# Storing one expert's result in sixteen row blocks instead of three, in a one-core mixture-of-experts kernel on Trainium2

## The chip, the cores and the metric

The kernel runs on one core of one Trainium2 chip. Its time is that of one execution on the device, in microseconds. Before the change two timed runs took 182.07 and 181.54 us, with a median of 181.81. The core has five engines with instruction streams of their own: TensorE (PE, whose weight loads are shown as PEld), VectorE (DVE), ScalarE (ACT), GpSimd (POOL) and SyncE (SP). Transfers run on 16 DMA engines that the core's queues share; SyncE, ScalarE and GpSimd issue them.

## The reference

Eight experts, each a two-layer network on its own 256 tokens, all in float32:

```python
n_experts, capacity, hidden, expert_hidden = 8, 256, 512, 2048
h = np.matmul(x, w1) + b1[:, np.newaxis, :]
h = np.maximum(h, 0)
return (np.matmul(h, w2) + b2[:, np.newaxis, :]).astype(np.float32)
```

The output is 8 x 256 x 512 floats, 512 KB for each expert.

## The kernel before

The work goes expert by expert. `first_product` (line 114) computes the hidden layer of an expert in 16 blocks of 128 units, four matmuls each (line 121), and ScalarE applies bias and ReLU on the way out of PSUM (line 128). `second_product` (line 166) runs three experts later (`LAG = 3`): for each of the two token blocks a bias matmul with a row of ones (line 171) and 16 matmuls (line 178). Experts 6 and 7 (`HALVED`) take their second weights in two halves of 1 MB, so that the products of the first half can start before the second has landed.

The weights are loaded as float16 by GpSimd's queue, which casts on the way (lines 84 and 93). The order of GpSimd's issues is written out by hand in a list, `ring` (lines 215 to 225), and is the order in which its queue moves data: activations, first weights, second weights, and at the end, behind the last weights, the grouped stores (`flush`, line 138).

`store` (line 142) copies an expert's two PSUM blocks to SBUF, one by VectorE (line 156), one by ScalarE (line 157). Each of the 128 rows of the tile is 4 KB, contiguous in the output. Where the result goes from there depends on the expert:

- Experts 0 to 3 and experts 4 and 5 are gathered in two tiles, which GpSimd's queue stores at the end in one transfer of 2 MB and one of 1 MB (line 140).
- Expert 6 is stored at once, in the row ranges that the table `PARTS` (line 40) gives: rows 0 to 25 by SyncE, 25 to 121 by ScalarE, 121 to 128 by SyncE (line 164).
- Expert 7, which is not in the table, is stored by SyncE in one transfer of 128 rows (line 164).

Instructions of one engine run in the order of the program. On ScalarE the copy of expert 7 (line 157) stands behind the issues for expert 6 (line 164); on SyncE the store of expert 7 stands behind those of expert 6. The two loads of the first two experts' activations (line 190) are SyncE's as well. The framework that builds the kernel gives the transfers of SyncE and ScalarE eight semaphores in turn; when one comes round again, the issue waits for the transfer that had it before.

Of the kernel before, what the change touches and what calls it, by code (L numbers as in the profile page):

```python
# [10 lines left out]
def kernel(  # L11
# [12 lines left out]
    E, T, H = x.shape  # L24
    M = w1.shape[2]
    P = 128
# [10 lines left out]
    HALVED = (E - 2, E - 1)  # L37


    PARTS = {E - 2: ((0, 25, False), (25, 121, True), (121, 128, False))}  # L40
    nXF32 = 2
    X_LOADS = {2: 2, 4: 4}

# [98 lines left out]
    def store(e, po):  # L142
# [16 lines left out]
        if e in group_of:  # L159
            if e == first + n - 1:  # L160
                pending[first] = (dst, out_sb)
            return
        for p0, p1, scalar in PARTS.get(e, ((0, P, False),)):
            (nc.scalar if scalar else nc.sync).dma_start(out=dst[p0:p1], in_=out_sb[p0:p1])
# [101 lines left out]
```

## Time and profile before

| | |
|---|---|
| time, median of two runs | 181.81 us (181.54 to 182.07) |
| span of the profiled execution, first to last instruction | 179.8 us (no other time is recorded for it) |
| mean granted TensorE clock | 0.932 |
| HBM read and written | 71.39 MB and 4.19 MB, 420 GB/s over the span |
| DMA packets | 3828, of them 460 under 512 B |
| costliest group: first product, line 121 | 512 matmuls, 64.9 us busy |
| second product, line 178 | 256 matmuls, 60.0 us busy |
| copies of results, lines 156 and 157 | 22 each, 15.1 and 12.7 us busy |

How to read the views that follow: the page lists busy time by engine and cuts the span into 40 slices, each digit a busy share in tenths. The queue rows give packets, megabytes and the time that the packets took as a share of 16 engines' span; q0 is GpSimd's queue, q1 SyncE's and q10 ScalarE's. The chain of waits gives start, duration and what ran or was waited for, in order of time. The DMA view lists issues with size and the time from issue to landing; it can be cut to a stretch of time, and its shares are then shares of that stretch. The windows give busy time of each engine, the granted clock, the DMA share and GB/s for chosen stretches. Times in the views count from the span's start.

### The profile page before, as it was taken

What the parts mean: (1) busy time and instruction counts of PE and PEld (TensorE: products, weight loads), DVE (VectorE), ACT (ScalarE), POOL (GpSimd) and SP (SyncE); (2) the same over time, 40 slices, a digit from 0 to 9 for tenths busy, and PEclk for the clock granted to TensorE, in tenths of its full rate; (3) what the DMA queues carried; (4) which work ended last, traced back from release to release, by engine and by line L of the source; (5) the groups of instructions that cost most, each with busy time, mean ns of one, the idle gap of its engine ahead of it and who ended that gap; (6) DMA issues with size and microseconds to landing.
All of it is one profiled execution on the core that took longest, in us unless ns stands there. A gap on an engine that the chain in (4) does not pass through costs nothing.

```text
span 179.8 us, 1957 instructions
## 1 busy us (share of the span) xinstructions
PE 129.0 (72%) x784; PEld 86.2 (48%) x784; DVE 87.8 (49%) x125; ACT 70.2 (39%) x151; POOL 13.4 (7%) x28
## 2 busy tenths in 40 slices
PE   0005199959995930999869597969788887999740
PEld 0004089948993410794369244943387433343310
DVE  1999933985000199999999998000600020301010
ACT  0000569947993050482189005940298020111010
POOL 7000003020201010001000001000100020020000
PEclk9999999987999995599999799996999999999995
DMA  5999999999999999999999999999999999999995
GB/s 215 252 230 195 233 208 201 233 228 200 215 231 193 219 230 222 197 226 230 208 204 230 219 200 226 230 211 200 230 219 201 226 211 208 217 211 221 324 456 215
DMA packets 3828, 40.56 MB, mean 226 GB/s; under 512 B 460, under 2 KB 476, under 8 KB 1132
## 3 DMA queue, kind: packets, MB, share of 16 engines
q0 software_dynamic: 3232, 38.35, 96.5%
q1 hardware_dynamic: 476, 1.70, 2.4%
q10 hardware_dynamic: 112, 0.39, 0.5%
q8 instruction: 6, 0.10, 0.2%
q14 instruction: 2, 0.02, 0.0%
HBM read 71.39 MB, written 4.19 MB: 420 GB/s over the span
## 4 chain that ended last, share of the span: by engine, by line
DMA 55%; PE 32%; ACT 3%; another core or an unknown queue 3%; POOL 2%; issue 1%; POOLq 0%; ACTq 0%
DMA w1sb<-in_w_dram 43%; PE po L178 16%; PE ph L121 15%; DMA w2sb<-in_w_dram 12%; ACT out L157 3%; PE po L171 1%; POOL w1sb L84 1%; ACT hT L128 1%; POOL w2sb L93 0%; POOL x L76 0%; POOL b_sb L192 0%; POOL b_rows L196 0%; POOLq L250 0%; ACTq L128 0%
## 5 line engine op out<-in xcount | busy, mean ns | idle before, releaser
L121 PE MATMUL ph<-xT,w1sb 128*128 128x256 f16 x512 | 64.9, 293 | 34.1 <-DMA w1sb<-in_w_dram 21.5
L121 PEld LDWEIGHTS <-w1sb 128*128 128x128 f16 x512 | 59.8, 147 | 40.1 <-DMA w1sb<-in_w_dram 31.8
L178 PE MATMUL po<-w2sb,hT 128*128 128x512 f16 x256 | 60.0, 394 | 9.8 <-DMA w2sb<-in_w_dram 9.8
L112 DVE STREAM_TRANSPOSE xT<-x 32x256 f16<-32x256 f16 (+1 forms) x64 | 53.0, 888 | 26.0 <-DMA x<-in_x_dram 19.2
L128 ACT ACTIVATE hT<-ph,b1T 128x256 f16<-128x256 f32 x128 | 56.2, 474 | 14.4 <-PE ph L121 14.2
L178 PEld LDWEIGHTS <-hT 128*128 128x128 f16 x256 | 25.5, 101 | 44.1 <-issue 17.8
L156 DVE COPY out<-po 32x512 f32<-32x512 f32 (+2 forms) x22 | 15.1, 688 | 53.7 <-PE po L178 53.5
L157 ACT COPY out<-po 32x512 f32<-32x512 f32 (+2 forms) x22 | 12.7, 579 | 68.8 <-PE po L178 68.6
L109 DVE STREAM_TRANSPOSE xT<-x 32x256 f16<-32x256 f16 x32 | 14.0, 436 | 0.5
L93 POOL DMA_DIRECT2D w2sb<-in_w_dram x10 | 5.3, 534 | 71.6 <-PE po L178 71.6
L84 POOL DMA_DIRECT2D w1sb<-in_w_dram x8 | 4.8, 601 | 64.1 <-PE ph L121 63.3
L128 ACT ACT_TABLE_LOAD x1 | 1.3, 1283 | 20.1 <-DVE b1T L208 20.1
L171 PE MATMUL po<-b_sb,ones 1*128 1x512 f16 x16 | 4.8, 379 | 0.0
L208 DVE STREAM_TRANSPOSE b1T<-b_rows 32x512 f32<-32x512 f32 x4 | 4.1, 1031 | 0.1
L201 DVE CAST x<-x 128x1024 f16<-128x1024 f32 x2 | 1.4, 694 | 3.1 <-DMA x<-in_x_dram 3.1
L171 PEld LDWEIGHTS <-ones 1*128 1x128 f16 x16 | 0.9, 92 | 2.1 <-issue 2.1
L140 POOL DMA_DIRECT2D out_dram<-out x2 | 1.1, 538 | 9.8 <-ACT out L157 9.8
L76 POOL DMA_DIRECT2D x<-in_x_dram x2 | 1.1, 552 | 0.0
L197 DVE MEMSET ones<- 1x128 f16 x1 | 0.2, 165 | 0.8 <-PEq L250 0.8
L196 POOL DMA_DIRECT2D b_rows<-in_b_dram x1 | 0.5, 515 | 0.0
L192 POOL DMA_DIRECT2D b_sb<-in_b_dram x1 | 0.5, 513 | 0.0
L250 POOL MEMSET const-float32-0.0<- 128x1 f32 x1 | 0.1, 99 | 0.2 <-issue 0.2
(3 smaller groups left out, 0.3 us busy)
## 6 DMA issues: line engine op xcount, KB each, us to landing
w1sb<-in_w_dram POOLq DMA_DIRECT2D x8, 2048.0 KB, 34.8
w2sb<-in_w_dram POOLq DMA_DIRECT2D x6, 2048.0 KB, 47.2
w2sb<-in_w_dram POOLq DMA_DIRECT2D x4, 1024.0 KB, 23.2
out_dram<-out POOLq DMA_DIRECT2D x1, 2048.0 KB, 19.0
x<-in_x_dram SPq DMA_DIRECT2D x2, 512.0 KB, 3.7
x<-in_x_dram POOLq DMA_DIRECT2D x1, 1024.0 KB, 31.2
out_dram<-out POOLq DMA_DIRECT2D x1, 1024.0 KB, 14.9
x<-in_x_dram POOLq DMA_DIRECT2D x1, 512.0 KB, 24.0
```

The costliest lines, as they stand in the source:

```text
L84: ordered(nc.gpsimd.dma_start(out=w1_sb[e], in_=w1[e].rearrange("(p kc) m -> p kc m", kc=nKC)))
L93: ordered(nc.gpsimd.dma_start(out=w2_sb[e][:, lo : lo + half], in_=src[:, lo : lo + half]))
L109: nc.vector.transpose(out=out[:, :, g, :, 0, :], in_=block[:, :, :, 0, :])
L112: nc.vector.transpose(out=out[:, tb, g], in_=block[:, tb])
L121: ordered(nc.tensor.matmul(out=ph, lhsT=w1_sb[e][:, kc, :].rearrange("p (q j) -> p q j", j=nJ)[:, :, j], rhs=xT[e][:, kc, :], start=(kc == 0),
L128: nc.scalar.activation(out=hT[e][:, j, :].rearrange("p (tb k i) -> p tb k i", tb=nTB, k=split), in_=ph.rearrange("p (tb i k) -> p tb k i", ...
L156: nc.vector.tensor_copy(out=out_sb[at : at + rows, k * nTB, :], in_=po[0][part])
L157: nc.scalar.copy(out=out_sb[at : at + rows, k * nTB + 1, :], in_=po[1][part])
L171: ordered(nc.tensor.matmul(out=t, lhsT=ones1, rhs=b2_sb[0:1, e * H : (e + 1) * H], start=True, stop=False,))
L178: ordered(nc.tensor.matmul(out=po[tb], lhsT=hT[e][:, j, tb * P : (tb + 1) * P], rhs=w2_sb[e][:, j, :], start=False, stop=(j == nJ - 1),))
L201: nc.vector.tensor_copy(out=t, in_=x32[e])
L208: nc.vector.transpose(out=b1T[b * B : (b + 1) * B, nB - 1 - b : nB - 1 - b + nJ * B], in_=b1_rows.rearrange("r (i j) -> r j i", j=nJ),)
```

## The change

The table entry of expert 6 is replaced. Instead of three transfers of 25, 96 and 7 rows there are sixteen, of 15, 8, 13, 14, 11, 12, 9, 10, 7, 6, 5, 4, 3, 2, 1 and 8 rows, SyncE and ScalarE in turn beginning with SyncE. They cover the same 128 rows in order. In words: the store of expert 6 in sixteen transfers of 1 to 15 rows, so that every DMA engine gets its own count of rows.

```diff
-    PARTS = {E - 2: ((0, 25, False), (25, 121, True), (121, 128, False))}
+    RUNS = ((15, False), (8, True), (13, False), (14, True), (11, False), (12, True), (9, False),
+            (10, True), (7, False), (6, True), (5, False), (4, True), (3, False), (2, True),
+            (1, False), (8, True))
+    PARTS = {E - 2: []}
+    for rows, scalar in RUNS:
+        at = PARTS[E - 2][-1][1] if PARTS[E - 2] else 0
+        PARTS[E - 2].append((at, at + rows, scalar))
+    assert PARTS[E - 2][-1][1] == P
```

Nothing else is edited; lines below the table move down by seven. The built instruction streams of PE, DVE and POOL keep their order. Those of SP and ACT become, from the first store on (rows x elements, and the semaphores of DMA transfers that the issue waits for; semaphores of engines are left out):

```
SP    store 15x1024
SP    store 13x1024
SP    store 11x1024
SP    store  9x1024   waits DMAHW1 (an activation load had it)
SP    store  7x1024   waits DMAHW3 (the 15-row store)
SP    store  5x1024   waits DMAHW5 (the 13-row store)
SP    store  3x1024   waits DMAHW7 (the 11-row store)
SP    store  1x1024   waits DMAHW1 (the 9-row store)
SP    store 128x1024  waits DMAHW2 (the 6-row store), and both copies of expert 7
ACT   store  8x1024
ACT   store 14x1024
ACT   store 12x1024
ACT   store 10x1024
ACT   store  6x1024   waits DMAHW2 (the first 8-row store)
ACT   store  4x1024   waits DMAHW4 (the 14-row store)
ACT   store  2x1024   waits DMAHW6 (the 12-row store)
ACT   store  8x1024   waits DMAHW0 (the 10-row store)
ACT   copy of expert 7's second block, line 157 (before the change it stood behind one store)
```

Which transfer had a semaphore before is read off the order in which the eight are given out. In the kernel before, no issue of a store waited for another transfer.

## Prediction

> **What bounds the kernel now.** I read the page first (busy shares and queues), then the chain of waits for its last steps, then the timeline of the issuing queues, and last the DMA view and the windows over the end.
>
> ```profile
> span 179.8 us, 1957 instructions
> ...
> PE 129.0 (72%) x784; PEld 86.2 (48%) x784; DVE 87.8 (49%) x125; ACT 70.2 (39%) x151; POOL 13.4 (7%) x28
> ...
> DMA  5999999999999999999999999999999999999995
> ...
> q0 software_dynamic: 3232, 38.35, 96.5%
> q1 hardware_dynamic: 476, 1.70, 2.4%
> q10 hardware_dynamic: 112, 0.39, 0.5%
> ...
> DMA 55%; PE 32%; ACT 3%; another core or an unknown queue 3%; POOL 2%; issue 1%; POOLq 0%; ACTq 0%
> ```
>
> The 16 DMA engines are full in every slice but the first and the last; no compute engine is above 72%. GpSimd's queue (q0) fills them with weights, and at the end with two grouped stores. Whatever lengthens the work of the busiest DMA engine, or issues the last transfer later, can move the end.
>
> ```profile
> 147.74 21.57 DMA w2sb<-in_w_dram
> 169.32 0.04 issue
> 169.36 3.63 PE po L178 x16
> 172.99 0.02 issue
> 173.01 0.59 ACT out L157
> ```
>
> The last compute chain: the last weights land at 169.32, 16 matmuls follow, then ScalarE copies the second half of expert 7 from 173.01 to 173.60. SyncE then issues the last store. The DMA view gives the stores and what they took to land, the timeline their issues:
>
> ```profile
> out_dram<-out POOLq DMA_DIRECT2D x1, 2048.0 KB, 19.0
> ...
> out_dram<-out POOLq DMA_DIRECT2D x1, 1024.0 KB, 14.9
> ...
> out_dram<-out SPq DMA_DIRECT2D x1, 512.0 KB, 5.3
> out_dram<-out ACTq DMA_DIRECT2D x1, 384.0 KB, 8.1
> out_dram<-out SPq DMA_DIRECT2D x1, 100.0 KB
> ...
> out_dram<-out SPq DMA_DIRECT2D x1, 28.0 KB
> ```
> ```profile
> L164 SPq DMA_DIRECT2D out_dram<-out x3: 301/358/360, 164.8 to 173.6; - x3
> ...
> L164 ACTq DMA_DIRECT2D out_dram<-out x1: 380/380/380, 164.8 to 164.8; - x1
> ```
>
> Expert 6's three stores are issued from 164.81 on, expert 7's store (512 KB) at 173.60, and it lands 5.3 later, at 178.9. Behind that come 0.9 us of closing steps, so the span ends at 179.8. No separate time of the profiled execution is recorded; the median of the two timed runs, 181.81, is 2.0 us above this span, and I carry that difference over unchanged.
>
> The windows over the end show how level the DMA engines finish (the columns before the last two are empty engines and the clock; the last but one is the DMA share, where a packet counts at its start):
>
> ```profile
> 177.00:178.56 1.56, 0.00 (x0) 0.00 (x0) 0.00 (x0) 0.00 (x0) 0.00 (x0) 0.50 0.57 234
> ```
> ```profile
> 177.20:177.40 0.20, 0.00 (x0) 0.00 (x0) 0.00 (x0) 0.00 (x0) 0.00 (x0) 0.50 0.90 369
> 177.40:177.60 0.20, 0.00 (x0) 0.00 (x0) 0.00 (x0) 0.00 (x0) 0.00 (x0) 0.50 0.65 266
> 177.60:177.80 0.20, 0.00 (x0) 0.00 (x0) 0.00 (x0) 0.00 (x0) 0.00 (x0) 0.50 0.70 287
> 177.80:178.00 0.20, 0.00 (x0) 0.00 (x0) 0.00 (x0) 0.00 (x0) 0.00 (x0) 0.50 0.80 328
> 178.00:178.20 0.20, 0.00 (x0) 0.00 (x0) 0.00 (x0) 0.00 (x0) 0.00 (x0) 0.50 0.27 103
> 178.20:178.40 0.20, 0.00 (x0) 0.00 (x0) 0.00 (x0) 0.00 (x0) 0.00 (x0) 0.50 0.10 41
> 178.40:178.60 0.20, 0.00 (x0) 0.00 (x0) 0.00 (x0) 0.00 (x0) 0.00 (x0) 0.50 0.00 0
> ```
>
> In the last 1.56 us an engine idles 43% of the time: 0.67 us. That is the most that perfect levelling could win. About 11 of 16 engines (0.70) work to 178, five have stopped by 177.6.
>
> **The change, part by part.** It removes three issues (25, 96 and 7 rows) and adds sixteen. Nothing moves on TensorE, VectorE and GpSimd: their built instruction order is the same.
>
> *Rows per engine.* q1's 1.70 MB are 416 rows of 4 KB (256 of the two x loads, 25, 7 and 128); its other 60 packets are small. The three 128-row transfers have 16 small ones each if they behave as q10's 96 rows (112 packets, 16 small); 12 are left, which is 5 + 7: 25 rows went to 5 engines and 7 rows to 7. So a transfer of r rows up to 15 gives one row to each of r engines. If all begin at the same engine, as the change's words have it, the loads were 12 rows on five engines, 7 on two, 6 on nine; they become 16, 15, 14, 13, 12, 11, 10, 9, 7, 6, 5, 4, 3, 2, 1, 0. The Trainium skill ("DMA: Bandwidth & Descriptors", section "Why a DMA increments its semaphore by 16 and not by 1") says that hardware queues take the lowest-numbered engines; no row here names an engine.
>
> *Price of a row.* In the last store's window:
>
> ```profile
> q1 hardware_dynamic: 144, 0.52, 45.8%
> ```
>
> This is 175.80 to 178.60: 45.8% of 16 engines times 2.8 us is 20.5 us, for 128 rows 0.160 us each. The heaviest engine gets 4 rows more, 0.64 us, and 13 more small packets (16 transfers for 3). Their price is not shown; the q10 row below (23.0% of 16 x 4.2 us over 96 rows: 0.161 us) hardly differs, so they lie between 0 and about 0.02 us: 0 to 0.26 in all. Which engines end early decides whether this shows. Starting level, the 11 light engines would end 0.8 to 0.96 us ahead of the five heavy; the windows show 11 late and five early. In the packet records behind these views the early five carry no q1 rows ahead of the last store, so they are light engines, and the heavy five are among the late eleven. These ends lie between about 177.9 and 178.55. The first gets 0.64 to 0.9 more: its new end is 178.55 to 179.45, **0 to +0.9 us**; I take +0.6. The rows taken off the upper engines free partly engines that were early already.
>
> *Issues and their waits.* ScalarE now issues 8 at 0.38 us, SyncE 9 with the last. The built listing says more: four of each go out at once, from 164.81 to 166.3. Each later one waits for the landing of the transfer four places ahead on its own queue (SyncE's 9-row one waits for an x load, long done). Behind ScalarE's last issue stands the copy of 173.01. The last store waits for ScalarE's 6-row transfer. Before, no such wait existed, so I bound it by the rings' pace:
>
> ```profile
> q0 software_dynamic: 107, 0.79, 99.7%
> ```
> ```profile
> q0 software_dynamic: 154, 1.29, 72.3%
> q10 hardware_dynamic: 112, 0.39, 23.0%
> q1 hardware_dynamic: 41, 0.13, 7.7%
> ```
>
> The first is 164.81 to 168.36: for 3.55 us after the issue only q0 moves. The second is 168.30 to 172.50: all 7 packets per engine of q10 pass among q0's. From the landing, (8.1 - 3.55) / 7 = 0.65 us per packet; from the window, 4.1 / 7 = 0.59. I take 0.62. A one-row transfer is two packets, so the n-th of a queue has landed near 168.4 + 1.24 n: 169.6, 170.9, 172.1, 173.4.
> - ScalarE: the 6-row issue goes at 169.6, the last 8-row one at 173.4, done 173.8. The copy starts there and not at 173.01: +0.8, done 174.4.
> - SyncE: its four later issues go at the same marks, the last done by 173.8.
> - The 6-row transfer, issued until 170.0, is fifth on its ring: landing 174.6, or by the issue delay 170.0 + 3.55 + 1.24 = 174.8. So the last store goes at 174.8, **1.2 us late**.
>
> What that costs at the end is bounded by two landings, the loaded 5.3 above and the shortest of the idle x loads:
>
> ```profile
> DMA to landing us min/median/max: 3.3/3.7/4.1
> ```
>
> 174.8 + 3.3 = 178.1 (hidden behind q0's last packets) and 174.8 + 5.3 = 180.1 (+1.2). The cover is q0, which in the old run was still writing the grouped stores when the store was issued:
>
> ```profile
> q0 software_dynamic: 61, 1.00, 105.9%
> ```
>
> That is 173.60 to 175.80, nothing but q0. An issue in 174.8 comes as q0 runs dry, so it is nearer the idle end: I take 4.6, which is 179.4, +0.5.
>
> *A rule against the change.* The Trainium skill ("DMA: Bandwidth & Descriptors", "Anatomy of one DMA" and "Rules for kernel authors") puts a fixed cost near 2.0 us on every DMA and says to merge what is under 64 KB. Fully in series, eight on ScalarE would be 16 us by its figure, and the copy would begin about 181, an estimate that adds some 8 us. The rows say that packets of one ring follow at 0.6 us without waiting for landings, which bounds the same eight by some 9 us, beside other work.
>
> **Sum.** The later of the two, not both added: +0.6 by rows, +0.5 by the late store. They fall partly on the same engines (the one with 16 rows takes the last store behind them), so I add a little: **+0.8 us**, span 180.6, time 181.81 + 0.8 = **182.6 us**.
>
> **The rivals.**
> 1. *Levelled, faster.* If the heavy five are in truth the early ones, or the upper engines are the latest, the staircase takes up to the 0.67 us of idling: 181.81 - 0.6 = 181.2. It decides only if the store is not issued much after 173.6 + 1.0. Against it: the eleven late ones hold the heavy group.
> 2. *Hidden.* Late issues lie behind q0, and the heaviest engine has been an early one: 181.8, within 0.2. The same comes out if the one-row transfers do not begin at the same engine, so that the staircase is none.
> 3. *ScalarE's copy stuck.* If each ring packet must let a 16 KB packet of q0 pass (105.9% of 16 x 2.2 us over 61 is 0.61 us), the pace is 0.61 + 0.16 = 0.77 us: the fourth landing is 168.4 + 8 x 0.77 = 174.6, the copy ends at 175.6, the 6-row transfer lands near 176.1, the store is 2.5 late: +0.5 to +2.5, about 184.0. For it: q0 goes to 16 KB packets in this stretch. Against it: 7 packets got through in 4.1 us.
> 4. *In series.* If the second four on ScalarE each took an idle landing of 3.3 one after the other, the copy would come at 169.6 + 13.2 = 182.8 instead of 173.0: +9.8 at most with no cover gained, about 190. Its q0 cover would be gone, so the last store lands in 3.3 and some 2.0 come back: 189.6. The skill's fixed price is of this kind. Against it: the listing has them wait for earlier transfers, not for each other.
>
> **How the numbers follow.** Forecast 0.51 (its own range 182.0 to 183.4), levelled 0.13, hidden 0.16, copy stuck 0.18, in series 0.02. The range 181.3 to 184.2 leaves out most of the levelled case's lower half, the upper part of the stuck copy and the series case: 0.2 together. About 2% (3.6 us) is what a measurement of this kernel can tell from no change. Faster by that needs more than all the idling there is: 0.01. Slower by that is the series case and the far end of the third: 0.04. Within: 0.95.
>
> **What would show it.** The last store's issue: 174.8 forecast (173.6 hidden, 176.1 stuck). ScalarE's last copy: 173.8 (173.0, 175.0). Sixteen store issues with gaps on both queues from 166.3 to about 169.6. Over the end, fewer engines busy in the last half microsecond than now, with a longer thin tail; for the levelled rival a share near 1 until a sharp drop. q1 and q10 together should show 128 more small packets less 28. Wrong would be: a copy on time and a store at 173.6, a wait on another transfer than the 6-row one, or an end that moves while both stay.

## The result and the profile after

The changed kernel took 182.66 and 185.04 us, a median of 183.85 against 181.81: a ratio of 1.012, 95% interval [1.0086, 1.0154]. That is slower, and within 2%. The profiled execution is the one of 182.66, its span 180.8 us, 1.0 more than before.

The two times differ by 2.4 us, so the kernel was run again. In all, 11 executions exist: six between 182.50 and 183.30 and five between 184.07 and 185.05. The profile of after shows one of the first kind, and they are told apart below.

The page of after: the packets and the two hardware queues.

```profile
span 180.8 us, 1971 instructions
...
DMA packets 3928, 40.56 MB, mean 224 GB/s; under 512 B 560, under 2 KB 576, under 8 KB 1232
...
q1 hardware_dynamic: 560, 1.84, 2.7%
q10 hardware_dynamic: 128, 0.26, 0.4%
```

There are 560 small packets for 460: 128 in place of 28, one for each row. q10's 0.26 MB are 64 rows and its other 64 packets are small. Each transfer of up to 15 rows did go to as many DMA engines as it has rows.

The end of the chain of waits of after (start, duration, what ran or was waited for):

```profile
164.22 0.59 ACT out L164
...
166.19 0.03 issue
166.22 7.87 DMA out_dram<-out
174.09 0.02 issue
174.11 0.28 ACTq L171
174.40 0.04 issue
174.44 0.02 ACTq L164
174.45 0.04 issue
174.49 0.58 ACT out L164
```

Before, the last copy followed the matmuls, at 173.01. Now it follows ScalarE's last issue, and that a transfer issued by 166.2 that landed at 174.09: the 10-row one, as the list of waits has it. The matmuls were done at 172.97. The issues of both queues (least, median and most ns; first and last start):

```profile
L171 SPq DMA_DIRECT2D out_dram<-out x9: 227/361/1753, 164.8 to 176.3; - x9
L171 ACTq DMA_DIRECT2D out_dram<-out x8: 276/392/1835, 164.8 to 174.1; - x8
```

The last store went out at 176.3, 2.7 us later than before; an issue can now take 1.8 us. The windows over the end, to be held against those of before:

```profile
176.50:177.00 0.50, 0.00 (x0) 0.00 (x0) 0.00 (x0) 0.00 (x0) 0.00 (x0) 1.00 0.33 139
177.00:177.20 0.20, 0.00 (x0) 0.00 (x0) 0.00 (x0) 0.00 (x0) 0.00 (x0) 1.00 0.36 143
...
178.20:178.40 0.20, 0.00 (x0) 0.00 (x0) 0.00 (x0) 0.00 (x0) 0.00 (x0) 0.52 1.00 410
178.40:178.60 0.20, 0.00 (x0) 0.00 (x0) 0.00 (x0) 0.00 (x0) 0.00 (x0) 0.50 0.67 266
178.60:178.80 0.20, 0.00 (x0) 0.00 (x0) 0.00 (x0) 0.00 (x0) 0.00 (x0) 0.50 0.41 164
178.80:179.00 0.20, 0.00 (x0) 0.00 (x0) 0.00 (x0) 0.00 (x0) 0.00 (x0) 0.50 0.15 61
179.00:179.20 0.20, 0.00 (x0) 0.00 (x0) 0.00 (x0) 0.00 (x0) 0.00 (x0) 0.50 0.10 41
```

Two things stand side by side. From 176.5 to 177.2 two thirds of the engines are idle: they wait for the late store. And after 178.6, where the kernel before was done, a shrinking group goes on for 0.6 us: by the prediction, the engines with the most rows. Which of the two sets the end is the question of the experiments.

### The profile page after: what moved, and what is told of

It is laid out like the page before. It is cut to its first block, busy times and chain, and to the rows that moved or that the text cites. A ratio compares the mean times of both kernels' runs of the same rounds, so it can differ in the third digit from the quotient of the medians.

```text
span 180.8 us, 1971 instructions
## 1 busy us (share of the span) xinstructions
PE 127.6 (71%) x784; PEld 85.5 (47%) x784; DVE 87.7 (49%) x125; ACT 70.1 (39%) x151; POOL 13.4 (7%) x28
## 4 chain that ended last, share of the span: by engine, by line
DMA 71%; PE 20%; POOL 2%; another core or an unknown queue 1%; issue 1%; ACTq 1%; ACT 1%; POOLq 0%
DMA w1sb<-in_w_dram 44%; DMA w2sb<-in_w_dram 23%; PE po L185 12%; PE ph L128 8%; DMA out_dram<-out 4%; ACTq L171 1%; POOL w1sb L91 1%; ACT out L164 1%; PE po L178 1%; POOL b_rows L203 0%; POOL b_sb L199 0%; POOL x L83 0%; ACTq L164 0%; POOLq L257 0%
## 5 line engine op out<-in xcount | busy, mean ns | idle before, releaser
L128 PE MATMUL ph<-xT,w1sb 128*128 128x256 f16 x512 | 63.6, 289 | 36.5 <-DMA w1sb<-in_w_dram 24.4
L128 PEld LDWEIGHTS <-w1sb 128*128 128x128 f16 x512 | 59.1, 147 | 41.8 <-DMA w1sb<-in_w_dram 34.6
```

The costliest lines, as they stand in the source:

```text
L128: ordered(nc.tensor.matmul(out=ph, lhsT=w1_sb[e][:, kc, :].rearrange("p (q j) -> p q j", j=nJ)[:, :, j], rhs=xT[e][:, kc, :], start=(kc == 0),
```

## The experiments

Theory R: the end is set by the DMA engines with the most rows; the late store is absorbed. Theory S: it is set by the late store. Later two more are needed: W, the waits add a cost that varies from execution to execution, and RW, both R and W.

**The changed kernel again.**

> The changed kernel again, to fix its time. Theory R (rows): the end is set by the DMA engines that got most rows of expert 6, the later last store is absorbed. Theory S (late store): the end is set by expert 7's store being issued 2.7 us later (176.3 for 173.6). Both expect the last copy of ScalarE near 174.5, the last store near 176.3, a span of 180.6 to 181.0 and a time 0.4 to 0.7% above the kernel before. If the time is about 1.2% above, as two earlier runs had it in the mean, something else is added that neither theory has.

Measured: 1.0116 [1.0071, 1.016], six executions from 182.50 to 185.05; copy at 174.0 in the profile, span 180.7. The short executions are as expected; that the mean is 1.2% above means that something is added that neither theory has.

**Rows without the wait.** In the program the transfers that are left after the first eight stand behind expert 7's. In the stream that was built, those of 7, 6 and 5 rows still go out ahead of expert 7's copy and store, at 170.2 to 171.1, and the last five, of 4, 3, 2, 1 and 8 rows, behind them.

```diff
+        if e in PARTS:
+            parts, held[:] = parts[:8], parts[8:]
+        else:
+            parts += held
```

> All sixteen transfers and their rows stay, but the last ones are put behind expert 7's copies and store in the program, so that neither the copy nor the store waits for the 10-row or the 6-row transfer. Both theories: copy at 173.0, store issued near 173.6. Theory R: the heaviest engines still carry 16 and 15 rows, span 180.4 to 180.9. Theory S: back to the span before, 179.7 to 180.0.

Measured: 1.0052 [1.0033, 1.0072], six executions from 182.72 to 183.10; span 181.0. The copy is at 173.25, and the store's issue in the timeline of SyncE is 0.3 us later than before:

```profile
173.86 0.36 SPq L177 DMA_DIRECT2D out_dram<-out  x1
```

After 178.6 a few engines go on, as in the changed kernel:

```profile
178.60:179.20 0.60, 0.00 (x0) 0.00 (x0) 0.00 (x0) 0.00 (x0) 0.00 (x0) 0.50 0.14 55
```

The time is not back. The rows cost 0.5%, 0.9 us, and without the wait of the copy there is no long execution among the six. One reservation: the last store had landed on all engines at 179.23, and the last landing of all, at 179.76, is that of a one-row transfer issued behind it, so a little of the 0.9 us may be the late issue of those five.

**The late store without the rows.**

```diff
-            nc.scalar.copy(out=out_sb[at : at + rows, k * nTB + 1, :], in_=po[1][part])
+            for _ in range(5 if e == E - 1 else 1):
+                nc.scalar.copy(out=out_sb[at : at + rows, k * nTB + 1, :], in_=po[1][part])
```

> The kernel before with its three transfers, but ScalarE copies expert 7's second block five times instead of once (same data to the same place), which moves the last store from 173.6 to about 176.0 and leaves the rows of expert 6 as they were. Theory R: the engines are busy with grouped stores to about 177 anyway, the last store lands within 0.2 us of 178.9, span 179.8 to 180.0. Theory S: span 180.5 to 182.2.

Measured: 1.0004 [0.9992, 1.0016]; span 179.9. Issues, and the windows of the end:

```profile
L165 SPq DMA_DIRECT2D out_dram<-out x3: 302/348/361, 164.9 to 176.3; - x3
```
```profile
176.50:177.20 0.70, 0.00 (x0) 0.00 (x0) 0.00 (x0) 0.00 (x0) 0.00 (x0) 0.50 0.26 105
177.20:178.40 1.20, 0.00 (x0) 0.00 (x0) 0.00 (x0) 0.00 (x0) 0.00 (x0) 0.50 1.00 406
178.40:178.60 0.20, 0.00 (x0) 0.00 (x0) 0.00 (x0) 0.00 (x0) 0.00 (x0) 0.50 0.19 62
```

The last store leaves at 176.3, as in the changed kernel, and the engines idle before it as there. Then all 16 write its 8 rows side by side and end at 178.6, as before. So S falls for this lateness: with the old rows, 2.7 us are absorbed. Before, the store was issued at 173.6, into engines that were full, and took 5.3 us; here it meets idle ones. The shortest landing of line 165 is that of the last store:

```profile
DMA to landing us min/median/max: 2.6/6.0/9.3
```

Issued at 176.32, it has landed at 178.96, against 178.88 before. So 2.7 us is about all that can be absorbed: 178.9 less 2.6 is 176.3, and a store that leaves later than that should move the end by as much. At this same issue time the changed kernel's last store has landed on ten engines by 178.99 and on the last at 179.64, so its rows cost 0.7 us, beside the 0.9 us of the version with the copy ahead.

**More skew, no waits.**

```diff
+    PARTS = {E - 2: ((0, 25, False), (25, 50, True), (50, 75, False), (75, 100, True), (100, 128, False))}
```

> Five transfers that wait for nothing (four of 25 rows and one of 28): 22 rows on five DMA engines, 2 on nine, none on two, where the kernel before has 12, 7 and 6. Copy at 173.0 and store near 173.6 under every theory. Theory R: ten rows more at 0.16 us on engines that ended among the last, 1.2 to 1.6 us, span 180.8 to 181.5, all executions alike. Theory W alone: no waits, so the time of the kernel before, within 0.3 us.

Measured: 1.008 [1.0059, 1.0101], 183.04 to 183.55; span 181.3. After 178.6:

```profile
178.60:180.00 1.40, 0.00 (x0) 0.00 (x0) 0.00 (x0) 0.00 (x0) 0.00 (x0) 0.50 0.22 88
```

For 1.4 us a fifth of the engines work alone (0.22 of 16 on average). Ten rows more on five engines made 1.45 us (0.8% of 181.65), 0.145 for each. R's price of a row holds.

**A level split.**

```diff
+    PARTS = {E - 2: [(16 * i, 16 * i + 16, i % 2 == 1) for i in range(8)]}
```

> The store of expert 6 in eight transfers of 16 rows, SyncE and ScalarE in turn: 8 rows on every DMA engine, no issue before the copy waits for a landing. Both theories: copy at 173.0, store near 173.6. Theory R: the five engines that had 12 rows end 0.6 us earlier, the late ones among those that had 6 get 2 rows, 0.32 us, more: span 179.5 to 180.1. Theory S: 179.7 to 179.9. It shows whether a plain level split is better than both tables.

Measured: 1.0033 [1.0019, 1.0047], 182.02 to 182.93; span 181.0 in the profile. R as I had put it was too hopeful: 8 rows on every engine is worse than 12, 7 and 6.

```profile
177.40:177.60 0.20, 0.00 (x0) 0.00 (x0) 0.00 (x0) 0.00 (x0) 0.00 (x0) 0.50 1.03 430
177.60:177.80 0.20, 0.00 (x0) 0.00 (x0) 0.00 (x0) 0.00 (x0) 0.00 (x0) 0.50 0.36 143
...
179.00:179.20 0.20, 0.00 (x0) 0.00 (x0) 0.00 (x0) 0.00 (x0) 0.00 (x0) 0.50 0.20 82
```

Ten engines end by 177.6 and about six run on to 179.2. With equal rows this gap must come from what ran before, and the landings on record show it coming. In the kernel before, a weight transfer lands at 162.77 to 163.55 on ten engines and at 163.92 to 164.17 on six. The number of late ones grows through the run, 3 at 61 us, 4 at 90, 5 at 109 and 6 at 139, and each of these three steps follows a packet of 16 KB on q8, the queue for instructions, at 83.9, 105.7 and 134.8 (0.94 to 0.95 us each). That such a packet holds one engine back for good is argued from these times; no run tested it. The six seem not to be the five heavy ones: in the skewed version, whose five heavy engines have 22 rows, the last store lands on five engines by 177.42, on six at 177.93 to 178.24 and on five at 179.84 to 180.35. So the table of the kernel before, which gives few rows to the late six, counters a part of this. This profile was one in which expert 6 finished 1.65 us late (its issues began at 166.5), so its own numbers are no measure of the mean.

**Sixteen transfers, level.** Half rows, so that each engine's bytes are those of the level split.

```diff
+    PARTS = {E - 2: [(16 * i, 16 * i + 16, False) for i in range(8)]}
...
+            for r in ((0,), (1,)) if e in PARTS else ((0, 1),):
+                (nc.scalar if scalar else nc.sync).dma_start(
+                    out=dst[p0:p1, r[0] : r[-1] + 1], in_=out_sb[p0:p1, r[0] : r[-1] + 1])
+                scalar = not scalar
```

> Every DMA engine gets the same bytes as with eight transfers of 16 rows, but in sixteen transfers (16 rows, half a row wide each), SyncE and ScalarE in turn, so that ScalarE's last copy again stands behind issues that wait for landings and the last store waits for one too. Nothing but the number of transfers and the waits differs from the eight. Theory R (rows alone set the end, the waits are absorbed): the time of the eight transfers, 182.3 to 182.7, with a spread like theirs. Theory W (the waits add a cost that varies from execution to execution): copy at 173.5 to 176, single times up to 184 or 185, median 0.5 us or more above the eight.

Measured: 1.0054 [1.0034, 1.0074], 182.19 to 183.47, copy at 175.25 in the profile. The copy is stuck by 2.2 us, yet no execution reached 184, and the interval overlaps that of the eight transfers. Inconclusive: the two differ by 0.4 us, which the intervals do not separate, and W's long executions did not appear; why not stays open. One reason may be that the stuck copy let the last store go at 175.9, ahead of the 176.3 up to which lateness was free above. The pair is also not as clean as was expected: the packets are of 2 KB, twice as many as those of 4 KB there, and SyncE's stores start 1.6 us earlier in this version, at 163.2, since half rows need VectorE's copy alone.

**Looking for a long execution.**

> The changed kernel once more, to see in a profile what its executions near 184 to 185 us do: four of eight so far were at 184.0 or above and four between 182.5 and 182.9. Theory W: in a long execution the copy of ScalarE starts at 175.5 or later and the last store is issued at 177.5 or later. Theory R: copy and store as in the profile at hand, and the extra time lies elsewhere.

> The same as the run before it, a second chance to profile an execution of 184 us or more; if both are short, this one shows how much the copy's start (174.0 and 174.5 so far) varies between short executions.

Measured: 183.25 and 183.30, both spans 181.5, for different reasons. The first is near the profile of after, with the copy at 174.56 and the store at 176.77, 0.4 us later; one engine ran on alone at the end, and its last landing came at 180.27, 0.5 us after all others. Why is open. In the second, expert 6's own copy came at 165.83, not 164.2. TensorE works in order, and the second product of the expert before, expert 5, had run 8.75 us and not 7.07, which moved expert 6's own to 158.71:

```profile
149.50 8.75 PE L185 MATMUL po<-w2sb,hT 128*128 128x512 f16 x32 [2.09 <-DMA w2sb<-in_w_dram]
```
```profile
158.28 1.17 ACT L164 COPY out<-po 64x512 f32<-64x512 f32 x2 [10.20 <-PE po L185]
165.83 0.59 ACT L164 COPY out<-po 128x512 f32<-128x512 f32 x1 [6.38 <-PE po L185]
```

The product at 149.50 is copied in blocks of 64 rows, as a grouped expert's is; the next one, copied at 165.83, is expert 6's. (The expectation of the next experiment takes the product on the slow clock for expert 6's own.) The windows of that stretch, in two profiles of the changed kernel (clock third from the end), after first:

```profile
149.50:156.57 7.07, 7.00 (x32) 3.03 (x32) 1.38 (x2) 0.35 (x1) 0.49 (x1) 1.00 1.04 218
```
```profile
149.50:156.57 7.07, 7.07 (x25) 2.87 (x25) 1.38 (x2) 0.00 (x0) 0.00 (x0) 0.76 1.04 217
```

At a granted clock of 0.76 for 1.00, 25 matmuls fit where 32 did. Within it the clock is 0.50 for some three microseconds:

```profile
150.00:151.00 1.00, 1.00 (x5) 0.42 (x4) 0.00 (x0) 0.00 (x0) 0.00 (x0) 0.66 1.17 246
151.00:152.00 1.00, 1.00 (x4) 0.30 (x2) 0.00 (x0) 0.00 (x0) 0.00 (x0) 0.50 0.94 197
152.00:153.00 1.00, 1.00 (x4) 0.36 (x3) 0.00 (x0) 0.00 (x0) 0.00 (x0) 0.50 1.02 213
153.00:154.00 1.00, 1.00 (x5) 0.36 (x4) 0.00 (x0) 0.00 (x0) 0.00 (x0) 0.64 1.10 229
```

The losses add to 0.34 + 0.50 + 0.50 + 0.36 = 1.7 us, the lateness seen. The Trainium skill ("TensorE: Matmul & The Clock Gate", "Part 1: The HAM clock gate") has the clock at half speed by default and after an idle window of about 3.4 us, in windows that run freely and do not start with the kernel. Depth and length agree: the clock on record in this trace is 0.50 for 3.41 us from 150.31. The idle stretch ahead does not: it was 2.09 us, so here less than such a window was enough, and the kernel before has as long a stretch there without the dip. The profile of after has such a dip too, one product earlier, on expert 4's:

```profile
139.89 8.75 PE L185 MATMUL po<-w2sb,hT 128*128 128x512 f16 x32 [1.52 <-DMA w2sb<-in_w_dram]
```

There it cost nothing, since expert 5's product had to wait for its weights until 149.5 anyway. What puts the dip on one product or the other is open. In the execution of 183.30 the whole chain then came 1.7 us later: copy at 176.26, last store at 177.7, and nearly nothing moved before the store:

```profile
177.50:178.30 0.80, 0.00 (x0) 0.00 (x0) 0.00 (x0) 0.00 (x0) 0.00 (x0) 0.58 0.06 21
178.30:179.80 1.50, 0.00 (x0) 0.00 (x0) 0.00 (x0) 0.00 (x0) 0.00 (x0) 0.50 0.86 350
```

All engines run dry, and the store sets the end: it left 1.3 us after the free 176.3 and had landed at 180.32, 1.4 us later than in the kernel before. So the late store does bind, when expert 6 is late.

**A late expert 6, made on purpose** in three kernels by copying its second block five times.

```diff
-            nc.scalar.copy(out=out_sb[at : at + rows, k * nTB + 1, :], in_=po[1][part])
+            for _ in range(5 if e == E - 2 else 1):
+                nc.scalar.copy(out=out_sb[at : at + rows, k * nTB + 1, :], in_=po[1][part])
```

First the changed kernel:

> The changed kernel with ScalarE's copy of expert 6's second block done five times (same data, same place), so that all sixteen issues start 2.4 us later, at 167.2, as they do by 1.65 us in the profile whose second product of expert 6 ran on a halved TensorE clock. Theory RW (rows set the end in an even execution; when expert 6 is late, the chain of waits carries all of the lateness to the last store, and the DMA engines run dry): copy at 176.5 to 177.5, last store at 178.2 to 179.2, all DMA engines idle for half a microsecond or more before it, span 182.2 to 183.5, time 184.0 to 185.5. Theory R alone: the time of the changed kernel's short executions, 182.5 to 183.3.

Measured: 1.0165 [1.0148, 1.0183], four executions from 184.03 to 184.93; in the profile (where the clock dipped too, so that the first copy began at 166.25) the last copy is at 178.61, the store at 179.2, and the engines are dry:

```profile
179.50:180.00 0.50, 0.00 (x0) 0.00 (x0) 0.00 (x0) 0.00 (x0) 0.00 (x0) 0.50 0.03 8
180.00:180.50 0.50, 0.00 (x0) 0.00 (x0) 0.00 (x0) 0.00 (x0) 0.00 (x0) 0.50 0.91 369
```

Every execution is long now. The same lateness in the kernel before:

> The same 2.4 us of lateness put into the kernel before. Nothing in it waits for the landing of expert 6's stores. Theory RW: copy at 173.0, last store at 173.6, the lateness is hidden behind the grouped stores, time 181.6 to 182.3. If lateness of expert 6 costs by itself (its rows pile up on the engines at the end): 182.5 or more.

Measured: 1.0013 [0.9999, 1.0026], store issued at 173.8, hidden. And in the version with the copy ahead of the last issues:

> The same lateness put into the version that has all sixteen transfers but issues the last of them behind expert 7's copies and store. Theory RW: copy near 173.0 and the store by 175, so only the rows cost: 182.6 to 183.3, no execution above 183.6. If it is at 184 or above, the lateness is dear for sixteen transfers even without the wait of the copy.

Measured: 1.0093 [1.0067, 1.012], median 183.01, five executions from 182.72 to 183.37 and one at 184.48 that the expectation had excluded; copy at 172.94 in the profile. Taking the copy out of the wait removes most of the cost of the lateness, 1.75 us of the medians, and not the rare long execution, whose cause is open.

**A long execution, profiled.**

> The changed kernel a last time, for a profile of an execution of 184 us or more (four of ten so far). Theory RW: if long, expert 6's first copy on ScalarE starts 3 us or more later than 164.2, the last copy at 177 or later, and the DMA engines are idle before the last store. If it is long while expert 6 is on time, the long executions have another cause.

Measured: 184.85 us, span 183.1. The chain and the windows:

```profile
165.87 0.59 ACT out L164
166.46 0.02 issue
166.48 6.50 DMA out_dram<-out
172.98 0.02 issue
173.00 5.53 DMA out_dram<-out
178.53 0.04 issue
178.57 0.59 ACT out L164
```
```profile
178.00:178.50 0.50, 0.00 (x0) 0.00 (x0) 0.00 (x0) 0.00 (x0) 0.00 (x0) 0.50 0.02 8
...
179.50:180.00 0.50, 0.00 (x0) 0.00 (x0) 0.00 (x0) 0.00 (x0) 0.00 (x0) 0.50 0.01 0
180.00:180.40 0.40, 0.00 (x0) 0.00 (x0) 0.00 (x0) 0.00 (x0) 0.00 (x0) 0.50 1.00 399
```

Expert 6 was late by the same 1.65 us (165.87), not by 3; the copy and the dry engines are as RW has them. By the semaphores on record, the first landing of the chain is that of the first 8-row transfer, and the second that of the 6-row one, for which the last store waits. What holds the copy is ScalarE's last issue: it waits for the 10-row transfer, issued at 169.94 and landed at 178.17, and the copy behind it starts at 178.57. The store then leaves at 179.2, finds all engines idle and has landed at 181.85, 2.7 us later. Why 1.65 us of lateness became 4.1 us at the copy here and 1.8 in the execution of 183.30 is not settled. A part of it is that ScalarE's third issue took 2.2 us here and 1.1 there, so that the 10-row transfer went out 1.3 us later; why the issue took longer is open.

## Why the prediction was right, and where it was not

- *Direction, size and range.* 182.6 was forecast; 183.85 is the middle of a short and a long execution, 183.3 the median of all 11, and 182.5 to 183.3 are the short ones, which the forecast had in mind. Slower by less than 2% was its likeliest case.
- *Rows.* The row's price of 0.160 us was right (0.145 in the skewed version). The term was taken at +0.6 of 0 to 0.9 and measures 0.9 (the version with the copy ahead, which holds its last five transfers behind the last store) or 0.7 (landings at equal store time): near its upper end. It was reasoned rightly that the heavy engines were among the late ones.
- *Pace of the rings.* Mis-sized. The 10-row transfer was to land at 173.4 and the copy to start at 173.8; they came at 174.1 and 174.5. The store was to go at 174.8 and went at 176.3. The pace of the third rival, one 16 KB packet ahead of each ring packet, gave 174.6 and 176.1, which is nearer: the mean pace was taken from a stretch in which most of q0's packets were 8 KB.
- *Cost of the late store.* Also mis-sized, the other way: +0.5 for 1.2 us of lateness, and 2.7 us cost 0.1 (interval of the ratio 0.9992 to 1.0016) when expert 6 is on time. The step was the landing on engines that run dry: taken as 4.6, between bounds of 3.3 and 5.3, it measures 2.6, below both. So the end stays until the store leaves after 176.3 and moves with it from there. That the store came later than forecast and cost less nearly cancels in the short executions, which is luck.
- *Fails: all executions alike.* The forecast argued from one profile, in which expert 6 was on time. The waits tie the last store to expert 6's finish, which came 1.65 us late, by the granted clock, in two of its five profiles; the kernel before hides such lateness. The third rival had the copy and the store held by the waits, at +0.5 to +2.5, but by a slower pace of the rings in every execution and not by a late expert 6 in some. Five of 11 executions were long, at 2.3 to 3.2 us above the median before. One of the five was profiled, and its store left 5.6 us late. For the other four this cause is not shown: a late expert 6 also gave a short execution, 183.30.
- *What was to be seen.* Sixteen issues, 100 more small packets, the thin tail at the end: all there. The store did wait for the 6-row transfer, as forecast: it was issued at 170.0, its last landing is on record at 176.26, and the store's issue follows at 176.34.
- *Level rival.* Levelling is not to be had this way: 16, 15, 14 ... 0 is skew, 8 each is worse too, with six engines late from the loads, and 12, 7 and 6 was the best split tried. No version here beats the kernel before.

## What to carry to other kernels

Where several DMA engines drain to a common end, price a split by the engine that gets most and by how late each engine arrives, not by equal bytes. An issue that waits for a landing must not stand, on an in-order engine, ahead of work that the end needs: in one profile it costs nothing, and in the next it passes a microsecond of clock variation on to the end. Before trusting a single profile, look at what can be late in another execution and which waits would carry it.

## What was not expected of the hardware

A last store issued 2.7 us later can be free: it took 5.3 us to land when it was issued into full engines at 173.6, and 2.6 us on idle ones at 176.3. A DMA issue of expert 6's or 7's stores, 0.30 to 0.38 us in the kernel before, took up to 1.8 us in the changed one, and 2.3 us in the long execution. The 10-row transfer, issued at 166.2 behind three others of its queue and beside GpSimd's full one, landed 7.9 us later; which of the two made it so long was not tested.
